# An earlier o product, wider stacked transfers and shorter layer norm sums in the first mixer of a hybrid decoder step

## The chip, the cores and the metric

The kernel runs on one core of one Trainium2 chip. The metric is the device time of one execution in microseconds (us). The time before is 1579.87 us, the median of three runs (1579.34 to 1582.29). All input weights and activations are float32.

## The reference

One inference step of a decoder trunk, for a prompt of 512 tokens and 8 samples of 8 tokens each, 576 tokens in all, d_model 1024. There are two layers, each a mixer and a convolutional FFN. The change is in the mixer of layer 0 alone:

```python
a_val, a_gate, q, k, v = split(h @ w_in)
u = a_val * sigmoid(a_gate)
c = silu(layernorm(causal_dwconv([conv_hist, u], conv_w, conv_b), ln_g, ln_b))   # 512 channels, 31 taps
q, k = partial_rope(rmsnorm(q)), partial_rope(rmsnorm(k))
o = sink_attention(q, k, v)          # window 128, 8 query heads, 2 key heads of 64
out = concatenate([c, o]) @ w_out    # 512 + 512 rows, 1024 columns
x = x + out
...
def layernorm(x, g, b):              # over the 512 channels of a token
    mu = mean(x); var = mean((x - mu)**2)
    return (x - mu) * rsqrt(var + EPS) * g + b
```

The second mixer (a Mamba-2 scan) and the two FFNs follow it and are not touched.

## The kernel before

Activations are kept with channels on the 128 partitions and tokens along the row: a tile is 128 x 576, and `HALF` names its two halves of 288 tokens. One matmul handles 128 channels of input, 128 of output, and one half.

Matmuls on weights are done with split operands. `weights()` loads 128 x 1024 weights on SP's queue (L141), ScalarE rounds them to a high part `wh` (L150), VectorE subtracts it to get the low part `wl` (L151). `split()` does the same for activations (L170 on ScalarE gives `oh`, L171 on VectorE gives `ol`). `mm3()` then issues three matmuls for each block of 128: L160 high by high, L161 high by low, L162 low by high. Results go through PSUM banks that come round in a ring, and `add_x` (L259, VectorE) adds them to the residual.

The mixer's work runs interleaved. `units()` projects the gate and value columns of the four channel blocks and q, k, v. The convolution of channel blocks 0 and 2 is done on VectorE, 31 operations of 128 x 576 for each block (`some_taps`, L436). Blocks 1 and 3 are done on TensorE by `pe_conv`: the block's `cap` (prompt) and `cas` (samples) are written to DRAM (`cad`) and read back so that four shifted copies of 32 channels stand on 128 partitions (`xp4`, `xs4`), and 64 + 64 small matmuls (L559, L566) sum the taps. `convs[1]` and `convs[3]` are these two, "conv1" and "conv3" in short. Attention goes block by block: `scores(n)` (TensorE, then the softmax on VectorE, ScalarE and GpSimd), `values(n)` (L648 transposes, L650 copies by ScalarE, L653 products, results to `of`), and `sample_scores` (L684, L688) and `sample_values` (L698 to L711) for the samples.

At the end of the mixer `of` is split into `oh` and `ol`, the layer norm of the convolution is formed from `ca[0..3]` (mean L758, variance L182, spread over the partitions L193), and the output product is done in two parts: `w_out_e[1]` times o, then `w_out_e[0]` times the normalized c, with the next norm begun in between.

A scheduler sets the order of the instructions on each engine when the program is built, from the order of the code, the dependences and its own estimates; engines then take their queues strictly in that order. All transfers stand in SP's queue, each one behind the completion of the transfer eight before it.

Of the kernel before, what the change touches and what calls it, by code (L numbers as in the profile page):

```python
# [8 lines left out]
F32 = mybir.dt.float32  # L9
# [3 lines left out]
ADD, SUB, MUL, MAX, MIN = ALU.add, ALU.subtract, ALU.mult, ALU.max, ALU.min  # L13

P = 128
NP = 512
T = 576
HB = 288
# [4 lines left out]
HALF = (slice(0, HB), slice(HB, T))  # L23
# [27 lines left out]
class Builder:  # L51
# [300 lines left out]
    def mix0(self):  # L352
        nc, d = self.nc, self.d
# [17 lines left out]
        cap, ca = {}, {}  # L371
# [3 lines left out]
        def a_gate(i):  # L375
            def go(half, p):
                if half == 0:
                    sg[i] = self.S("sg")
                    cap[i] = self.segp.tile([P, 542], F32, tag="capp", bufs=1, name="cap") if i in PC else self.S("cap", 542)
# [12 lines left out]
        cad = {i: self.dp.tile([P, 846], F32, name=f"cad{i}") for i in PC}  # L392

        def segment(i):

# [7 lines left out]
        def a_val(i):  # L403
            def go(half, p):
                s = sg[i]
                if half == 0:
                    nc.vector.tensor_tensor(cap[i][:, 30:318], p[:, :HB], s[:, :HB], op=MUL)
                else:
                    nc.vector.tensor_tensor(cap[i][:, 318:542], p[:, :224], s[:, HB:NP], op=MUL)
                    nc.vector.tensor_tensor(cas_v[i][:, :, 30:38], bt(p[:, 224:288]), bt(s[:, NP:]), op=MUL)  # L410
                    nc.sync.dma_start(d["ca_p"][i], cap[i][:, 512:542])
                    nc.sync.dma_start(d["ca_s"][i], cas_v[i][:, :, 8:38])
                    self.free(sg.pop(i))
                    if i in PC:
                        nc.sync.dma_start(cad[i][:, 0:542], cap[i])
                        nc.sync.dma_start(cad[i][:, 542:846].rearrange("p (b c) -> p b c", c=38), cas_v[i])
# [23 lines left out]
        def some_taps(n):  # L440
            for _ in range(n):
                next(taps, None)
# [94 lines left out]
        def pe_conv(i):  # L537
            w4 = [self.S("w4", NP) for _ in range(2)]
            for a in range(2):
                nc.gpsimd.tensor_tensor(w4[a].rearrange("p (k m) -> p k m", m=32),  # L540
                                        self.cv("m32", 0, 32).unsqueeze(1).broadcast_to([P, 16, 32]),
                                        self.pv("ca_wq", i * 32 + a * 16, 16).unsqueeze(2).broadcast_to([P, 16, 32]), op=MUL)
            xp4 = [self.S("xp4", 540) for _ in range(4)]
            xsp = [self.S("xs4", 608) for _ in range(2)]
            xs4 = [xsp[c // 2][:, (c % 2) * 304:(c % 2) * 304 + 304] for c in range(4)]
            src = cad[i]
            for c in range(4):
                for j in range(4):
                    n = 540 if j < 3 else 536
                    r, rc = slice(j * 32, j * 32 + 32), slice(c * 32, c * 32 + 32)  # L550
                    nc.sync.dma_start(xp4[c][r, 0:n], src[rc, j:j + n])
                    nc.sync.dma_start(xs4[c][r, 0:304 - j], src[rc, 542 + j:846])
            yield
            pp, ps = self.pm(), self.pm()
            for s in range(8):
                k = slice(0, P if s < 7 else 96)
                for c in (3, 2, 1, 0):
                    w = w4[s // 4][k, (s % 4 * 4 + c) * 32:(s % 4 * 4 + c) * 32 + 32]
                    m = nc.tensor.matmul(pp[c * 32:c * 32 + 32, :], w, xp4[c][k, 4 * s:4 * s + NP], start=s == 0, stop=s == 7)  # L559
                    if s or c < 3:  # L560
                        self.tc.keep_in_program_order(m)
            for s in range(8):
                k = slice(0, P if s < 7 else 96)
                for c in range(4):
                    w = w4[s // 4][k, (s % 4 * 4 + c) * 32:(s % 4 * 4 + c) * 32 + 32]
                    m = nc.tensor.matmul(bt(ps[c * 32:c * 32 + 32, 0:64]), w, xs4[c].rearrange("p (b t) -> p b t", t=38)[k, :, 4 * s:4 * s + 8],  # L566
                                         start=s == 0, stop=s == 7)
# [27 lines left out]
        of = []  # L595
# [81 lines left out]
        def sample_scores():  # L677
            for bh in range(2):
                p = [self.ps("sc", "sc") for _ in range(2)]
                for b4 in range(4):  # L680
                    b = bh * 4 + b4
                    for kv in range(2):
                        rows = slice(kv * 64, kv * 64 + 64)
                        nc.tensor.matmul(p[kv][b4 * 32:b4 * 32 + 32, 0:P], qs[rows, b * 32:b * 32 + 32],  # L684
                                         kct[bh][rows, b4 * P:(b4 + 1) * P], start=True, stop=True)
# [65 lines left out]
        lrs = self.S("lrs")  # L751
        csq = [self.S("csq") for _ in range(4)]
        cc = [self.pair("c") for _ in range(4)]
        for half in (0, 1):
            sl = HALF[half]
            pm = self.ps("pm")
            for i in range(4):
                nc.tensor.matmul(pm[:, :HB], self.o512, ca[i][:, sl], start=i == 0, stop=i == 3)  # L758
# [10 lines left out]
        self.free(oh, list(ca.values()), cas, lrs, csq)  # L769
# [465 lines left out]
def constants():  # L1235
# [3 lines left out]
    def put(name, a, i=0):  # L1239
        c[:a.shape[0], CV[name] + i:CV[name] + i + a.shape[1]] = a  # L1240
# [5 lines left out]
            prot[o + 8 + i, o + i] = -1.0  # L1246
            prot[o + i, o + 8 + i] = 1.0
    put("prot", prot)
    put("m32", np.tile(np.eye(32, dtype=f), (4, 1)))
# [132 lines left out]
```

## Time and profile before

| what | value |
| --- | --- |
| median of three runs | 1579.87 us |
| the profiled execution's own time | 1580.21 us |
| its span | 1578.4 us |
| TensorE's granted clock, mean | 0.997 |
| instructions | 28672 |

The profiled execution is 0.34 us above the median; 1.8 us of its time lie outside the span. Of a window's row the columns are: the window in us from the span's start, its length, then for each engine the busy time and in brackets the number of records, then the granted clock of TensorE as a share of full speed, the mean busy share of the DMA engines, and GB/s. A timeline's row has start, duration, engine, line, operation, result and operands with their shapes, the number of records, and in square brackets the idle time before the first of them and what ended it. PE is TensorE's matmul, DVE VectorE, ACT ScalarE, POOL GpSimd, SPq SP's queue of transfers.

### The profile page before, as it was taken

The page shows a single profiled execution, that of the slowest core. Times are in us where ns is not written, and L with a number is a line of the kernel's source. Part 1 is how long each engine was busy: PE and PEld are TensorE (multiplying, and loading weights), DVE is VectorE, ACT ScalarE, POOL GpSimd, SP SyncE. Part 2 cuts the span into 40 slices and gives each one's busy share as a digit, 9 for nine tenths or more (in the row PEclk, how much of TensorE's full clock was granted, in tenths as well). Part 3 has the DMA queues.
Part 4 walks back from the last instruction along what each step waited for, and adds up shares of the span by engine and source line. Part 5 has one row for each costly group of instructions (what it writes and reads, how often), then busy time and mean ns, then how long its engine had stood idle before and what let it go on. Part 6 is the DMA issues. An engine that isn't in the chain of part 4 may idle for free. (4 is left out here: it accounts for less than half of the span.)

```text
span 1578.4 us, 28672 instructions
## 1 busy us (share of the span) xinstructions
PE 1547.4 (98%) x11709; PEld 1478.0 (94%) x11709; DVE 997.7 (63%) x1750; ACT 642.0 (41%) x1197; POOL 146.9 (9%) x362
## 2 busy tenths in 40 slices
PE   8999999999999999999998999999999999999999
PEld 7966799999999999998997998998999999999998
DVE  7968586553465355677796777776975653653552
ACT  6257373221222122476765555556542321221220
POOL 0026001000000000011202002002010000000000
PEclk9999999999999999999999999999999999999999
DMA  7514223222222222225345235235322222222222
GB/s 224 127 43 111 75 69 103 87 88 81 81 80 82 93 78 76 78 83 162 122 123 163 94 106 178 94 110 171 112 81 81 81 81 81 89 77 91 81 84 76
DMA packets 69841, 157.60 MB, mean 100 GB/s; under 512 B 20158, under 2 KB 24510, under 8 KB 69710
## 3 DMA queue, kind: packets, MB, share of 16 engines
q1 hardware_dynamic: 69710, 155.77, 32.2%
q8 instruction: 92, 1.51, 0.4%
q14 instruction: 39, 0.32, 0.1%
HBM read 140.54 MB, written 15.21 MB: 99 GB/s over the span
## 5 line engine op out<-in xcount | busy, mean ns | idle before, releaser
L160 PE MATMUL mm<-hh,wh 128*128 128x288 f32 (+1 forms) x2288 | 681.6, 298 | 9.0 <-ACT wh L150 7.7
L162 PE MATMUL mm<-hh,wl 128*128 128x288 f32 x2288 | 679.9, 297 | 0.0
L161 PE MATMUL mm<-hl,wh 128*128 128x288 f32 (+1 forms) x2288 | 678.6, 297 | 0.0
L160 PEld LDWEIGHTS mm<-hh,wh 128*128 128x128 f32 (+1 forms) x2288 | 430.2, 188 | 15.1 <-ACT wh L150 8.2
L150 ACT ACTIVATE wh<-wr 128x1024 fp32r<-128x1024 f32 (+1 forms) x215 | 223.4, 1039 | 537.8 <-issue 265.4
L161 PEld LDWEIGHTS mm<-hl,wh 128*128 128x128 f32 (+1 forms) x2288 | 430.9, 188 | 2.0 <-DVE hl L360 0.3
L162 PEld LDWEIGHTS mm<-hh,wl 128*128 128x128 f32 x2288 | 429.8, 188 | 2.9 <-issue 1.5
L151 DVE TENSOR_TENSOR wl<-wr,wh 128x1024 fp32r<-128x1024 f32 (+1 forms) x215 | 259.8, 1209 | 81.5 <-ACT wh L150 81.3
L161 PE MATMUL mm<-yl,wh 128*128 128x288 f32 x960 | 287.0, 299 | 0.2 <-DVE yl L171 0.2
L160 PE MATMUL mm<-yh,wh 128*128 128x288 f32 x960 | 286.3, 299 | 0.7 <-DVE x L259 0.7
L162 PE MATMUL mm<-yh,wl 128*128 128x288 f32 x960 | 284.5, 297 | 0.4 <-DVE wl L151 0.4
L160 PEld LDWEIGHTS mm<-yh,wh 128*128 128x128 f32 x960 | 181.6, 190 | 4.3 <-DVE x L259 1.8
L161 PEld LDWEIGHTS mm<-yl,wh 128*128 128x128 f32 x960 | 182.0, 190 | 2.8 <-issue 1.4
L162 PEld LDWEIGHTS mm<-yh,wl 128*128 128x128 f32 x960 | 181.6, 189 | 1.6 <-issue 0.9
L259 DVE TENSOR_TENSOR x<-x,mm 128x288 f32<-128x288 f32 x192 | 85.3, 451 | 153.1 <-PE mm L162 152.8
L304 DVE TENSOR_TENSOR gbuf<-mm,rs 128x224 f32<-128x224 f32 x44 | 17.2, 391 | 108.9 <-PE mm L162 108.9
L315 ACT ACTIVATE gsilu<-gconv,par 128x512 f32<-128x512 f32 x44 | 31.8, 724 | 115.8 <-DVE gconv L312 115.8
L312 DVE SCALAR_TENSOR_TENSOR gconv<-gbuf,par,gconv 128x592 f32<-128x592 f32 x88 | 73.1, 831 | 1.5
L325 DVE TENSOR_TENSOR gsilu<-mm,gsilu 128x288 f32<-128x288 f32 x88 | 40.0, 455 | 50.7 <-PE mm L162 50.7
L801 DVE SCALAR_TENSOR_TENSOR cconv<-cbuf,par,cconv 128x600 f32<-128x600 f32 x72 | 60.2, 840 | 11.6 <-ACT cconv L799 10.7
L1022 ACT ACTIVATE acb<-acb,ac 128x128 f32<-128x128 f32 x128 | 41.4, 390 | 50.6 <-DMA acb<-acd 34.4
L307 POOL COPY fpo<-gbuf 128x2 f32<-128x2 f32 x44 | 12.4, 281 | 476.0 <-DVE gbuf L304 476.0
(306 smaller groups left out, 1603.1 us busy)
## 6 DMA issues: line engine op xcount, KB each, us to landing
wr<-in_w_gate SPq DMA_DIRECT2D x44, 512.0 KB, 3.3
wr<-in_w_up SPq DMA_DIRECT2D x44, 512.0 KB, 3.3
wr<-in_w_in_o SPq DMA_DIRECT2D x40, 512.0 KB, 3.4
wr<-in_w_down SPq DMA_DIRECT2D x32, 448.0 KB, 3.4
wr<-in_w_down SPq DMA_DIRECT2D x16, 512.0 KB, 3.6
acb<-acd SPq DMA_DIRECT2D x32, 256.0 KB, 4.2
h<-in_h SPq DMA_DIRECT2D x32, 256.0 KB, 3.7
out_ssm_s<-h SPq DMA_DIRECT2D x32, 256.0 KB, 2.4
```

The lines of the kernel that those rows point to most:

```text
L150: nc.scalar.activation(hi[:, :n], raw[:, :n], AF.Copy)
L151: nc.vector.tensor_tensor(lo[:, :n], raw[:, :n], hi[:, :n].bitcast(F32), op=SUB)
L160: nc.tensor.matmul(out, hi[:, ws], xh[:, sl], start=i == 0, stop=False)
L161: nc.tensor.matmul(out, hi[:, ws], xl[:, sl], start=False, stop=False)
L162: nc.tensor.matmul(out, lo[:, ws], xh[:, sl], start=False, stop=i == n - 1)
L259: nc.vector.tensor_tensor(self.x[m][:, sl], self.x[m][:, sl], p[:, :HB], op=ADD)
L304: nc.vector.tensor_tensor(g[:, 290:514], p[:, 0:224], rs[:, HB:NP], op=MUL)
L312: nc.vector.scalar_tensor_tensor(cv[:, :592], g[:, k:592 + k], w(k), cv[:, :592], op0=MUL, op1=ADD)
L315: nc.scalar.activation(sl[:, :NP], cv[:, :NP], AF.Silu, bias=b)
L325: nc.vector.tensor_tensor(sl[:, HALF[half]], p[:, :HB], sl[:, HALF[half]], op=MUL)
L801: nc.vector.scalar_tensor_tensor(cv[:, :600], g[:, k:600 + k], w(k), cv[:, :600], op0=MUL, op1=ADD)
L1022: nc.scalar.activation(acb[:, cs], acb[:, cs], AF.Relu, bias=ac[:, o:o + 1], scale=-1.0)
```

## The change

There are three parts, all in `mix0`.

First, the o product is broken up. `o_split(0)` splits the first 288 tokens of `of` ahead of the sample scores, `o_tile(m, 0)` forms output tile m for these tokens (m = 0, 1 after the sample scores, 2 to 5 after the last block's values), and the remaining tiles (m = 0 to 5 of the second half, 6 and 7 of both) come behind the layer norm's code, where all of it stood. Half 0 of `of` needs blocks 0 to 2 of the attention only.

Second, `pe_conv` reads the stacked input with 8 transfers of 128 partitions, where it had 32 of 32 partitions. Partition p now holds channel p // 4, shift p % 4; the tables `m32` and `taps4` are laid out to match, the last tap group runs over 128 rows instead of 96, and the tails of `cap` and `cad` are zeroed with two small transfers and memsets at the start.

Third, the layer norm's channel sums are made on VectorE first: `lsum` is the sum of the four `ca` tiles, and one matmul per half by `o512` gives the mean, where there were four; the squares are summed into `csq[0]`, and three variance matmuls per half replace twelve.

```diff
@@ segment tails
-                    cap[i] = self.segp.tile([P, 542], F32, ...)
+                    cap[i] = self.segp.tile([P, 543], F32, ...)
+                        nc.gpsimd.memset(cap[i][:, 542:543], 0.0)
...
+        zeros = self.Z("zeros", 3, bufs=1)
+        nc.gpsimd.memset(zeros, 0.0)
+        for i in PC:
+            nc.sync.dma_start(cad[i][:, 847:850], zeros)
@@ pe_conv
             for c in range(4):
-                for j in range(4):
-                    n = 540 if j < 3 else 536
-                    r, rc = slice(j * 32, j * 32 + 32), slice(c * 32, c * 32 + 32)
-                    nc.sync.dma_start(xp4[c][r, 0:n], src[rc, j:j + n])
-                    nc.sync.dma_start(xs4[c][r, 0:304 - j], src[rc, 542 + j:846])
+                for t, o, n in ((xp4[c], 0, 540), (xs4[c], 543, 304)):
+                    rows = cad[i][c * 32:c * 32 + 32, o:o + n]
+                    nc.sync.dma_start(t[:, 0:n], bass.AP(tensor=rows.tensor, offset=rows.offset,
+                                                         ap=[list(rows.ap[0]), [1, 4], [1, n]]))
@@ attention's end
+        oh = [self.pair("o") for _ in range(4)]
+        wo = {}
+        def o_tile(m, half):
+            if m // 2 not in wo:
+                wo[m // 2] = self.weights(d["w_out_e"][1, m // 2], 1024)
+            p = self.pm()
+            self.mm3(p[:, :HB], wo[m // 2], [(m % 2) * 4 + k for k in range(4)], oh, HALF[half])
+            self.add_x(m, half, p)
+        def o_split(half):
+            for j in range(4):
+                self.split(of[j][:, HALF[half]], oh[j], HALF[half])
+        o_split(0)
         sample_scores()
         next(convs[3])
         some_taps(5)
+        o_tile(0, 0)
+        o_tile(1, 0)
         values(3, p3)
         some_taps(5)
+        for m in range(2, 6):
+            o_tile(m, 0)
         sample_values()
         for _ in convs[3]:
             pass
         self.rings = {"mm": [2, 3, 0, 1], "aux": [4, 5, 6, 7]}
-        oh = [self.pair("o") for _ in range(4)]
-        for j in range(4):
-            self.split(of[j], oh[j])
+        o_split(1)
@@ layer norm, each half
-            for i in range(4):
-                nc.tensor.matmul(pm[:, :HB], self.o512, ca[i][:, sl], start=i == 0, stop=i == 3)
+            nc.vector.tensor_tensor(lsum[:, sl], ca[1][:, sl], ca[0][:, sl], op=ADD)
+            for i in (2, 3):
+                nc.vector.tensor_tensor(lsum[:, sl], lsum[:, sl], ca[i][:, sl], op=ADD)
+            nc.tensor.matmul(pm[:, :HB], self.o512, lsum[:, sl], start=True, stop=True)
...
                 nc.scalar.activation(csq[i][:, sl], ca[i][:, sl], AF.Square)
-            self.rstd(lrs, csq, self.o512[:, 0:1], sl)
+                if i:
+                    nc.vector.tensor_tensor(csq[0][:, sl], csq[0][:, sl], csq[i][:, sl], op=ADD)
+            self.rstd(lrs, csq[:1], self.o512[:, 0:1], sl)
...
-        self.out_proj([d["w_out_e"][1, c] for c in range(4)], oh, 4)
+        for m in range(6):
+            o_tile(m, 1)
+        for m in (6, 7):
+            for half in (0, 1):
+                o_tile(m, half)
```

The change also reorders the engines' queues. On TensorE, at the second group of sample scores (`kct` holds the samples' cached keys, `qss` their queries, `pt` transposed probabilities, `pm` the layer norm's mean, `o_101` the tile `o512`), the rows before are:

```order
L684 MATMUL sc<-kct,qss 32x128 [waits DVE_49]
L684 MATMUL sc<-kct,qss 32x128 x3
L688 MATMUL sc<-kf,qss 128x64
L648 MATMUL pt<-ident,sm 128x128 [waits Pool_49] x7
L758 MATMUL pm<-ca,o_101 128x288 [waits DVE_49]
L648 MATMUL pt<-ident,sm 128x128 [waits Activation_49]
L648 MATMUL pt<-ident,sm 128x128 x3
L758 MATMUL pm<-ca,o_101 128x288
L653 MATMUL po<-ptb,vt 64x512 [waits Activation_49]
```

After, at the same place on TensorE:

```order
L160 MATMUL mm<-oh,wh 128x288 [waits Activation_49]
L161 MATMUL mm<-ol,wh 128x288 [waits DVE_49]
L687 MATMUL sc<-kct,qss 32x128 [waits DVE_49]
L687 MATMUL sc<-kct,qss 32x128 x3
L691 MATMUL sc<-kf,qss 128x64
L162 MATMUL mm<-oh,wl 128x288
L160 MATMUL mm<-oh,wh 128x288 [waits Activation_49]
```

Eight o matmuls now stand ahead of these scores and sixteen more between them and the transposes of the last block's values (L651 after); the mean's matmuls are gone from here.

On VectorE, ahead of the sample softmax's first maximum (L605 before, L608 after; `cap` and `cas` are the gated values of channel block 3), the rows before are:

```order
L407 TENSOR_TENSOR cap<-mm,sg 128x288 [waits PE_49]
L436 SCALAR_TENSOR_TENSOR ca<-seg,par,ca 128x576 [waits DVE_49] x3
L409 TENSOR_TENSOR cap<-mm,sg 128x224 [waits PE_49]
L410 TENSOR_TENSOR cas<-mm,sg 128x8x8
L605 ISA sm,mx<-sc,cst 128x192 [waits PE_49,Pool_49]
L605 ISA mx 128x1
```

After, on VectorE:

```order
L171 TENSOR_TENSOR ol<-of,oh 128x288 [waits Activation_49,Pool_49]
L414 TENSOR_TENSOR cap<-mm,sg 128x288 [waits PE_49]
L171 TENSOR_TENSOR ol<-of,oh 128x288 [waits Activation_49,Pool_49] x2
L443 SCALAR_TENSOR_TENSOR ca<-seg,par,ca 128x576 [waits DVE_49] x2
L778 TENSOR_TENSOR lsum<-ca 128x288 [waits PE_49]
L416 TENSOR_TENSOR cap<-mm,sg 128x224 [waits PE_49]
L417 TENSOR_TENSOR cas<-mm,sg 128x8x8
L443 SCALAR_TENSOR_TENSOR ca<-seg,par,ca 128x576 [waits DVE_49]
L171 TENSOR_TENSOR ol<-of,oh 128x288 [waits Activation_49]
L608 ISA sm,mx<-sc,cst 128x192 [waits PE_49]
```

Four subtractions of the o split and the first add of `lsum` have come in ahead of the maximum; one tap (of the three that stood ahead of L407 before, by the counts from the preceding L151 on) has gone behind it.

On ScalarE, at the first projection of the mixer (`rs` is the reciprocal root of the first norm, `wh` the weights' high part), the rows before are:

```order
L184 ACTIVATE rs_r<-pt,eps 96x3 [waits PE_49] x2
L150 ACTIVATE wh<-wr 128x1024 [waits DMAHW1_49]
L197 ACTIVATE rs<-pr 128x288 [waits PE_49] x2
L150 ACTIVATE wh<-wr 128x1024 [waits DMAHW3_49,DVE_49]
L385 ACT_TABLE_LOAD
```

After, on ScalarE:

```order
L184 ACTIVATE rs_r<-pt,eps 96x3 [waits PE_49] x2
L197 ACTIVATE rs<-pr 128x288 [waits PE_49] x2
L150 ACTIVATE wh<-wr 128x1024 [waits DMAHW3_49]
L387 ACT_TABLE_LOAD
L387 ACTIVATE sg<-sg 128x288 [waits DVE_49] x2
```

The conversion that stood between L184 and L197 now follows the two copies of `rs`.

More of the change, by code (lines that the diff above doesn't have):

```diff
@@ L378, in go @@
                     sg[i] = self.S("sg")
-                    cap[i] = self.segp.tile([P, 542], F32, tag="capp", bufs=1, name="cap") if i in PC else self.S("cap", 542)
+                    cap[i] = self.segp.tile([P, 543], F32, tag="capp", bufs=1, name="cap") if i in PC else self.S("cap", 543)
+                    if i in PC:
+                        nc.gpsimd.memset(cap[i][:, 542:543], 0.0)
                     nc.gpsimd.memset(cap[i][:, 0:30], 0.0)
@@ L389, in mix0 @@
         segs = {}
+        zeros = self.Z("zeros", 3, bufs=1)
+        nc.gpsimd.memset(zeros, 0.0)
         PC, NPTB = (1, 3), 3
-        cad = {i: self.dp.tile([P, 846], F32, name=f"cad{i}") for i in PC}
+        cad = {i: self.dp.tile([P, 850], F32, name=f"cad{i}") for i in PC}
+        for i in PC:
+            nc.sync.dma_start(cad[i][:, 847:850], zeros)
         def segment(i):
@@ L414, in go @@
                     if i in PC:
-                        nc.sync.dma_start(cad[i][:, 0:542], cap[i])
-                        nc.sync.dma_start(cad[i][:, 542:846].rearrange("p (b c) -> p b c", c=38), cas_v[i])
+                        nc.sync.dma_start(cad[i][:, 0:543], cap[i])
+                        nc.sync.dma_start(cad[i][:, 543:847].rearrange("p (b c) -> p b c", c=38), cas_v[i])
                     else:
@@ L555, in pe_conv @@
             for s in range(8):
-                k = slice(0, P if s < 7 else 96)
                 for c in (3, 2, 1, 0):
-                    w = w4[s // 4][k, (s % 4 * 4 + c) * 32:(s % 4 * 4 + c) * 32 + 32]
-                    m = nc.tensor.matmul(pp[c * 32:c * 32 + 32, :], w, xp4[c][k, 4 * s:4 * s + NP], start=s == 0, stop=s == 7)
+                    w = w4[s // 4][:, (s % 4 * 4 + c) * 32:(s % 4 * 4 + c) * 32 + 32]
+                    m = nc.tensor.matmul(pp[c * 32:c * 32 + 32, :], w, xp4[c][:, 4 * s:4 * s + NP], start=s == 0, stop=s == 7)
                     if s or c < 3:
@@ L562, in pe_conv @@
             for s in range(8):
-                k = slice(0, P if s < 7 else 96)
                 for c in range(4):
-                    w = w4[s // 4][k, (s % 4 * 4 + c) * 32:(s % 4 * 4 + c) * 32 + 32]
-                    m = nc.tensor.matmul(bt(ps[c * 32:c * 32 + 32, 0:64]), w, xs4[c].rearrange("p (b t) -> p b t", t=38)[k, :, 4 * s:4 * s + 8],
+                    w = w4[s // 4][:, (s % 4 * 4 + c) * 32:(s % 4 * 4 + c) * 32 + 32]
+                    m = nc.tensor.matmul(bt(ps[c * 32:c * 32 + 32, 0:64]), w, xs4[c].rearrange("p (b t) -> p b t", t=38)[:, :, 4 * s:4 * s + 8],
                                          start=s == 0, stop=s == 7)
@@ L750, in mix0 @@
         some_taps(99)
-        lrs = self.S("lrs")
+        lrs, lsum = self.S("lrs"), self.S("lsum")
         csq = [self.S("csq") for _ in range(4)]
@@ L767, in mix0 @@
                 self.split(ca[i][:, sl], cc[i], sl)
-        self.out_proj([d["w_out_e"][1, c] for c in range(4)], oh, 4)
-        self.free(oh, list(ca.values()), cas, lrs, csq)
+        for m in range(6):
[3 more added lines that the diff above has]
+                o_tile(m, half)
+        self.free(oh, list(ca.values()), cas, lrs, lsum, csq)
         self.norm_begin("norm_f0", True)
@@ L1248, in constants @@
     put("prot", prot)
-    put("m32", np.tile(np.eye(32, dtype=f), (4, 1)))
+    put("m32", np.repeat(np.eye(32, dtype=f), 4, axis=0))
     half = np.arange(P) // 64
```

3 lines of the change are left out of this document (1 added, 2 removed).

## The prediction

> **What bounds the kernel now.** I read the engines' busy times first, then the chain that ended last, then the windows around the change, and only then single rows. The first two lines say that TensorE is busy for 98% of the span and that the chain's steps on an engine are nearly all its own.
>
> ```profile
> PE 1547.4 (98%) x11709; PEld 1478.0 (94%) x11709; DVE 997.7 (63%) x1750; ACT 642.0 (41%) x1197; POOL 146.9 (9%) x362
> PE 38%; DVE 2%; DMA 0%; ACT 0%; issue 0%; DVEq 0%; ACTq 0%
> ```
>
> So only two things can move the end: work taken from TensorE, and idle time of TensorE filled with work that it must do anyway. The windows show where the changed part has either. Their columns are sum, PE, PEld, DVE, ACT, POOL (busy us and records), granted clock, DMA share, GB/s.
>
> ```profile
> 147.96:184.57 36.61, 32.29 (x326) 21.02 (x325) 21.50 (x46) 11.71 (x32) 6.33 (x6) 0.95 0.38 83
> 184.57:206.94 22.37, 22.37 (x176) 21.75 (x177) 16.34 (x40) 15.96 (x33) 1.28 (x6) 1.00 0.14 48
> 150.00:160.00 10.00, 6.74 (x37) 3.86 (x37) 9.65 (x28) 5.86 (x15) 4.18 (x5) 0.83 0.56 90
> 300.00:320.00 20.00, 20.00 (x153) 20.00 (x152) 11.83 (x19) 5.16 (x7) 0.90 (x6) 1.00 0.24 81
> ```
>
> The first stretch (A) runs from the sample scores to the end of the last TensorE convolution ("conv3"), the second (B) on to the first matmul of c. A has the hole, at 150 to 160 with the clock down to 0.83; B is full, so there only removed work counts. The last row gives the yardstick: dense matmuls of 128x288 start every 20/153 = 0.131 us; I use 0.133.
>
> ```profile
> 149.43 0.33 PE L648 MATMUL pt<-ident,sm 128*128 128x128 f32 x1
> 150.21 0.42 PE L684 MATMUL sc<-kct,qss 64*32 64x128 f32 x8 [0.45 <-DVE mx L605]
> 150.92 0.98 PE L648 MATMUL pt<-ident,sm 128*128 128x128 f32 x7
> 156.37 1.88 PE L653 MATMUL po<-ptb,vt 128*64 128x512 f32 x4 [3.06 <-ACT ptb L650]
> 160.05 1.08 PE L653 MATMUL po<-ptb,vt 128*64 128x512 f32 x4
> 161.06 0.44 PE L698 MATMUL pt<-ident,sm 128*128 128x128 f32 x2
> 161.55 0.65 PE L758 MATMUL pm<-ca,o 128*128 128x288 f32 x2
> 162.13 0.44 PE L705 MATMUL po<-ptb,vts 64*64 64x128 f32 x4
> 163.08 0.44 PE L705 MATMUL po<-ptb,vts 64*64 64x128 f32 x4
> 165.34 0.53 PE L160 MATMUL mm<-oh,wh 128*128 128x288 f32 x2 [0.55 <-ACT oh L170]
> 176.59 7.08 PE L559 MATMUL mm<-xp,w 128*32 128x512 f32 x64
> 183.49 1.08 PE L566 MATMUL mm<-xs,w 128*32 128x64 f32 x64
> 206.94 0.29 PE L160 MATMUL mm<-ch,wh 128*128 128x288 f32 x1
> ```
>
> Before, TensorE has nothing to do while ScalarE copies the transposed probabilities (3.06 us), and the o product starts only at 165.34.
>
> **A, the o product in the hole.** Both kernels do 72 of the 192 o matmuls ahead of conv3 and 120 behind it, counted in the order of instructions, so the amount of this work is equal; its place moves by 16 us. What TensorE must do in A when nothing waits: sample scores from A's start to 149.43 and from 150.21 to 150.92, 1.46 + 0.71 = 2.17; 16 transposes by 0.107 (the third row's 0.98 less a fill, over 8) = 1.71; two value products at the rate of 160.05 to 161.06, 2.02; sample transposes 2 x 0.49 (161.06 to 161.55) and sample values 2 x 0.95 (162.13 to 163.08) = 2.88; 72 o matmuls by 0.133 = 9.58; conv3 from 176.59 to 184.57 = 7.98. Sum 26.34. The twelve mean records that before has here go (part B).
>
> To that come waits. The new one is at the second sample scores, queued on TensorE behind eight o matmuls, for a bank that VectorE's first maximum releases. Ahead of that maximum VectorE now does four o subtractions and one sum, and one tap fewer:
>
> ```profile
> 149.80 0.34 DVE L605 CUSTOM_DVE_ANT_0 sm<-sc,cst 128x192 f32<-128x192 f32 x1
> 206.54 0.82 DVE L171 TENSOR_TENSOR cl<-ca,ch 128x288 fp32r<-128x288 f32 x2
> 188.26 0.45 DVE L259 TENSOR_TENSOR x<-x,mm 128x288 f32<-128x288 f32 x1
> 146.17 3.28 DVE L436 SCALAR_TENSOR_TENSOR ca<-seg,par,ca 128x576 f32<-128x576 f32 x3
> 154.26 0.81 DVE L436 SCALAR_TENSOR_TENSOR ca<-seg,par,ca 128x576 f32<-128x576 f32 x1
> 138.42 9.34 POOL L616 TENSOR_SCALAR sm<-sm,den 128x256 f32<-128x256 f32 x8 [5.32 <-DVE den L614]
> ```
>
> 4 x 0.41 + 0.45 - 1.0 = 1.1 later, so the maximum ends near 151.2 to 151.7 and not at 150.14. TensorE is there at 149.43 + 8 x 0.133 = 150.5: a wait of 0.7 to 1.2, taken 1.1. What stands behind it (the second scores, then 16 o matmuls, then the transposes) moves along; nothing on ScalarE needs it sooner. The remaining waits (the sample probabilities' copies, the second value product) I set at 0.9, between nothing and what is left of before's: 36.61 less 26.34, less twelve mean records by 0.65/2, less the waits shown (3.06 + 0.45 + 0.55) and the 0.8 that the slow value product lost, 1.5. A then takes 26.34 + 2.0 = 28.4 in place of 36.61: **-8.2**.
>
> The rows of taps carry a choice. A tap takes 0.81 alone, and 3.28/3 = 1.09 while GpSimd's multiplications run, each 9.34/8 = 1.17. The five new two-input operations stand in that stretch too, so they cost up to 0.28 more each, 1.4 in all; that is the upper end of 1.1 to 1.6 in the step above. [...]
>
> **B, the layer norm's sums.** Removed from TensorE:
>
> ```profile
> L182 PE MATMUL pt<-o,csq x48: 164/223/244, 186.3 to 194.6; 128*96 128x1 f32 x48
> 188.17 1.61 PE L182 MATMUL pt<-o,csq 128*96 128x1 f32 x18
> 189.64 0.38 PE L162 MATMUL mm<-oh,wl 128*128 128x288 f32 x1
> L758 PE MATMUL pm<-ca,o x16: 405/406/510, 151.7 to 185.4; 128*128 128x288 f32 x16
> 184.54 1.24 PE L758 MATMUL pm<-ca,o 128*128 128x288 f32 x4
> 192.71 0.65 PE L193 MATMUL pr<-dg,ones 96*128 96x288 f32 x2
> ```
>
> A full-precision matmul stands as two records. The 48 variance records become 12; one takes (189.64 - 188.17)/18 = 0.082. The last four mean records stay as two halves of two, 1.1 together. B dense: 120 x 0.133 = 15.96, means 1.1, variances 12 x 0.082 = 1.0, the two spreads of rstd 2 x 0.5 (0.65 less a fill) = 1.0, sum 19.0; the same sum with 48 records gives 22.0 for a measured 22.37, so I add 0.4: 19.4, **-2.95**. VectorE gains five or six adds by 0.45 per half, of which one per half runs already in A. They lengthen the norm's chain, which TensorE covers with the 120 o matmuls. Before, the last c piece was ready at 206.54 + 0.82 = 207.36, that is 22.8 behind the end of conv3; after, the first tile of half 1 wants that piece 19.4 + 21 x 0.133 = 22.2 behind it. The chain loses 36 records and part of its waits behind TensorE, and gains up to 5 us of adds if none lies beside ScalarE's squares. Walking it with before's durations I get 22.0; the cost is 0 to 5.6, taken 0 since nearly every add stands beside a square.
>
> **The stacked taps.** 24 DMA issues go from SP's queue for each of the two convolutions.
>
> ```profile
> 156.52 0.32 SPq L551 DMA_DIRECT2D xp<-cad  x1
> 171.73 0.42 SPq L552 DMA_DIRECT2D xs<-cad  x1
> xp<-cad SPq DMA_DIRECT2D x12, 67.5 KB, 1.9
> cad<-cap SPq DMA_DIRECT2D x1, 271.0 KB, 5.6
> ```
>
> Before, 32 issues took 15.6 us and the last landed near 174, which conv3 at 176.59 did not feel. After, TensorE reaches conv3 near 169.0, so with the old transfers it would have had to wait 5 us: the wider ones pay here. They move 1.73 MB; the window of 150 to 160 shows 90 GB/s with the DMA engines 0.56 busy, 160 GB/s if full, so 11 us when nothing else runs and they land near 167.5. Cost 0, with some 1.5 us to spare.
>
> **The beginning.** The two small zero transfers stand early on SP's queue, ahead of the second pair of weight loads, and the scheduler moves one ScalarE conversion of gate weights behind two copies (L197).
>
> ```profile
> 15.01 1.85 SPq L141 DMA_DIRECT2D wr<-in_w_in_e  x2
> wr<-in_w_in_e SPq DMA_DIRECT2D x4, 512.0 KB, 6.7
> 23.98 1.05 ACT L150 ACTIVATE wh<-wr 128x1024 fp32r<-128x1024 f32 x1
> 25.06 1.23 DVE L151 TENSOR_TENSOR wl<-wr,wh 128x1024 fp32r<-128x1024 f32 x1 [0.41 <-ACT wh L150]
> 25.73 0.29 PE L162 MATMUL mm<-hh,wl 128*128 128x288 f32 x1
> ```
>
> Two issues of 0.9 move these loads to 16.86, and they land near 23.5 by the second row (which is of 10 to 24 us), just ahead of 23.98: 0, at most 1. The conversion now takes the slot of 23.98; its low part is done on VectorE at 25.06 + 1.23 = 26.29, and TensorE wants it at 25.73: **+0.65** (0 if ScalarE finds an earlier slot, 1.2 if the loads or the copies come later). Changes between kinds of matmul cost about 0.1 each in the rows of B (0.38 where 0.29 is normal); the new order has some eight more: **+0.8**.
>
> **Sum.** -8.2 - 2.95 + 0.65 + 0.8 = -9.7. The profiled execution took 1580.21, 0.34 above the median of the runs shown; 1580.21 - 9.7 = 1570.5. Bounds: waits in A from nothing to 3.5, hand-overs 0 to 1.5, beginning 0 to 1.2, which is a gain of 7 to 12.5 for this case, 1567.7 to 1573.2.
>
> **Rivals.** (1) Half the gain is lost on VectorE. Either each of the five new operations waits for a whole GpSimd instruction, 5 x 1.17 = 5.9 (1576.4), or the norm's adds all lie on its chain, 5.6 (1576.1). For it: VectorE is 9.65 of 10 busy at 150 to 160. Against it: taps lost 0.28 each, and 16 us of matmuls lie over the norm. 12%. (2) No change: both of these together, 11.5 against 9.7, so 1582. The step then only shifts its waits. 5%. (3) Slower: the wide transfers land late, and conv3, which stands in TensorE's queue ahead of the 120 remaining o matmuls, waits with nothing to cover it. It decides from a landing at 169.0 + 9.7 = 178.7, 22 us for eight transfers. If they went one by one at the pace of the last row above (5.6 for 271 KB), 1.73 MB would take 36 us, land at 192 and give 1594. Against it: 12 transfers of 67.5 KB landed in 1.9 each while issued 0.46 apart, so they overlap. 4%.
>
> **How the numbers follow.** The first case has 79%, and its middle is the prediction. The range 1566.5 to 1576.5 adds the upper rival's two prices and one us below for waits that the sum overstates; it leaves out (2), (3) and some of the tails, near 15%. A gain below 0.2%, 3.2 us, can't be told from no change here. Faster gets 0.90, from the first case and nearly all of (1), same 0.05, slower 0.05.
>
> **What the changed profile would show.** Right: the 3.06 wait at the value product gone; the first o matmul near 149.5; the granted clock of 150 to 160 near 1.0; a wait near 1 us on TensorE at the second sample scores; conv3 starting near 169 and the first c matmul near 197; 12 variance records; the eight wide transfers issued within 4 us and landed before 168. Wrong: a wait of TensorE ahead of conv3 for a DMA (3), waits at o matmuls for the subtraction or above 2 us at the scores (1), or idle time at the first c tiles for VectorE (1 and 2).

## The result, and the profile after

The changed kernel takes 1568.26 us (median of four runs, 1567.04 to 1569.66) against 1579.77 for the kernel before on the same chip; the ratio is 0.9928 with a 95% interval of 0.9914 to 0.9942, so 11.5 us faster where 9.4 were forecast (1570.5, range 1566.5 to 1576.5). The profiled execution took 1567.04 us with a span of 1565.3, 13.1 less than the profiled one of before.

The first fence has windows of the changed kernel: the prediction's stretches A (sample scores to the end of conv3) and B (to the first c matmul), then C (to the last c matmul), the ten microseconds that held the hole, and 340 us of dense work in the last FFN. The second fence has C and the dense work of the kernel before.

```profile
148.98:177.47 28.49, 28.13 (x313) 18.66 (x312) 22.82 (x54) 11.32 (x33) 7.90 (x7) 1.00 0.41 101
177.47:196.96 19.49, 19.03 (x140) 18.60 (x141) 18.11 (x45) 15.04 (x31) 0.30 (x3) 1.00 0.17 55
196.96:223.95 26.99, 26.94 (x204) 26.60 (x203) 23.30 (x52) 18.13 (x38) 1.72 (x11) 1.00 0.28 86
150.00:160.00 10.00, 9.68 (x80) 8.05 (x73) 9.55 (x30) 5.84 (x16) 5.52 (x6) 1.00 0.59 100
1205.00:1545.00 340.00, 340.00 (x2564) 339.80 (x2564) 172.26 (x265) 83.14 (x107) 8.78 (x52) 1.00 0.27 84
```

```profile
206.94:233.91 26.97, 26.86 (x204) 26.51 (x203) 22.58 (x50) 17.57 (x36) 0.88 (x8) 1.00 0.24 80
1218.00:1558.00 340.00, 340.00 (x2558) 339.79 (x2557) 171.79 (x263) 82.14 (x107) 8.76 (x52) 1.00 0.27 84
```

A fell from 36.61 to 28.49 (-8.1), B from 22.37 to 19.49 (-2.9), C is unchanged. A begins 1.0 later (148.98 against 147.96). That is 10.0 up to the last c matmul. The other 3.0 lie behind it, in layers that the change does not touch: six more matmuls fit into 340 us. The hole is gone and the clock there is 1.00, not 0.83.

TensorE's rows of the changed kernel: the wait at the beginning, what is left of waiting in the mixer, and the variance's records.

```profile
25.29 0.40 PE L162 MATMUL mm<-hh,wl 128*128 128x288 f32 x1 [0.46 <-DVE wl L151]
150.44 0.40 PE L160 MATMUL mm<-oh,wh 128*128 128x288 f32 x1
151.48 0.29 PE L161 MATMUL mm<-ol,wh 128*128 128x288 f32 x1
152.10 0.42 PE L687 MATMUL sc<-kct,qss 64*32 64x128 f32 x8 [0.33 <-DVE mx L608]
166.99 1.04 PE L563 MATMUL mm<-xp,w 128*32 128x512 f32 x2
177.93 0.75 PE L781 MATMUL pm<-lsum,o 128*128 128x288 f32 x2 [0.46 <-DVE lsum L780]
196.96 0.30 PE L160 MATMUL mm<-ch,wh 128*128 128x288 f32 x1
L182 PE MATMUL pt<-o,csq x12: 164/223/223, 182.6 to 188.7; 128*96 128x1 f32 x12
```

The o product starts at 150.44, 15 us sooner. The wide transfers, as the DMA view of 150 to 178, the view of their line (both convolutions) and SP's queue have them:

```profile
xp<-cad SPq DMA_DIRECT2D x4, 270.0 KB, 3.5
DMA to landing us min/median/max: 2.9/3.5/4.4
156.68 0.56 SPq L556 DMA_DIRECT2D xp<-cad  x1
161.50 0.60 SPq L556 DMA_DIRECT2D xs<-cad  x1
```

The last of the eight is issued at 161.50 and has the longest way, 4.4, so it lands at 165.9. Conv3 begins at 166.99 with two matmuls; the rest of it starts at 169.51, behind the sample values.

### The profile page after: what moved, and what is told of

It is laid out like the page before. It is cut to its first block, busy times and chain, and to the rows that moved or that the text cites. A ratio compares the mean times of both kernels' runs of the same rounds, so it can differ in the third digit from the quotient of the medians.

```text
span 1565.3 us, 28515 instructions
## 1 busy us (share of the span) xinstructions
PE 1538.9 (98%) x11661; PEld 1471.1 (94%) x11661; DVE 1002.2 (64%) x1766; ACT 642.3 (41%) x1201; POOL 148.5 (9%) x365
## 5 line engine op out<-in xcount | busy, mean ns | idle before, releaser
L162 PE MATMUL mm<-hh,wl 128*128 128x288 f32 x2288 | 681.5, 298 | 1.0 <-DVE wl L151 1.0
L161 PE MATMUL mm<-hl,wh 128*128 128x288 f32 x2288 | 678.2, 297 | 0.0
L162 PEld LDWEIGHTS mm<-hh,wl 128*128 128x128 f32 x2288 | 430.6, 188 | 4.8 <-issue 2.0
L161 PEld LDWEIGHTS mm<-hl,wh 128*128 128x128 f32 x2288 | 432.0, 189 | 2.6 <-DVE hl L171 0.6
L151 DVE TENSOR_TENSOR wl<-wr,wh 128x1024 fp32r<-128x1024 f32 (+1 forms) x215 | 260.1, 1210 | 82.0 <-ACT wh L150 81.9
L162 PE MATMUL mm<-yh,wl 128*128 128x288 f32 x960 | 283.3, 296 | 0.3 <-DVE wl L151 0.3
L162 PEld LDWEIGHTS mm<-yh,wl 128*128 128x128 f32 x960 | 180.4, 188 | 1.5 <-issue 0.9
```

The costliest lines, as they stand in the source:

```text
L151: nc.vector.tensor_tensor(lo[:, :n], raw[:, :n], hi[:, :n].bitcast(F32), op=SUB)
L161: nc.tensor.matmul(out, hi[:, ws], xl[:, sl], start=False, stop=False)
L162: nc.tensor.matmul(out, lo[:, ws], xh[:, sl], start=False, stop=i == n - 1)
```

## The experiments

The kernels of this section are given by their A, B and C windows. Between the first 15 us and the last matmul, a drop of the granted clock to one half lasts 3.41 us or a multiple of it in these traces (at 156.51, 842.59 and 1091.76 in the kernel before, at 738.04 and 847.27 in the changed one, each 3.41 at a clock of 0.50), and 3.41 cost up to 1.7. A window's loss by it is at most its length times what its clock lacks of 1.

**Each part taken out of the changed kernel, and each part put alone into the kernel before.**

```diff
@@ no_o, against after
-        o_split(0)
-        o_tile(0, 0)
...
+        for j in range(4):
+            self.split(of[j], oh[j])
...
+        self.out_proj([d["w_out_e"][1, c] for c in range(4)], oh, 4)
@@ no_transfers, against after
-                for t, o, n in ((xp4[c], 0, 540), (xs4[c], 543, 304)):
+                for j in range(4):
+                    nc.sync.dma_start(xp4[c][r, 0:n], src[rc, j:j + n])
+                    nc.sync.dma_start(xs4[c][r, 0:304 - j], src[rc, 542 + j:846])
@@ no_sums, against after
-            nc.tensor.matmul(pm[:, :HB], self.o512, lsum[:, sl], start=True, stop=True)
+            for i in range(4):
+                nc.tensor.matmul(pm[:, :HB], self.o512, ca[i][:, sl], start=i == 0, stop=i == 3)
-            self.rstd(lrs, csq[:1], self.o512[:, 0:1], sl)
+            self.rstd(lrs, csq, self.o512[:, 0:1], sl)
```

`transfers_alone`, `sums_alone` and `o_alone` are the kernel before with the second, the third and the first part of the change.

> The o product back behind the layer norm's code; the wide transfers and the summed layer norm stay. In this kernel's order the last convolution stands ahead of all 192 o matmuls, so nothing fills the hole ahead of the value product (3 us) but the convolution comes sooner. Theory: dense work up to the convolution's end is 26.3 - 9.6 = 16.8, plus some 7 us of waits, so it ends near 173 and the first c matmul follows 192 x 0.133 + 3.5 = 29 us later, near 202, against 196.96 in the changed kernel: some 5 us slower than it, near 1573.5. Rival: the early o product carries the whole 8.1 us of stretch A, then near 1576.5.

Measured: 1575.42 us (ratio to before 0.9963, 0.9948 to 0.9979).

```profile
150.07:176.45 26.38, 21.09 (x241) 9.95 (x240) 20.52 (x45) 11.77 (x32) 6.65 (x6) 0.81 0.42 108
176.45:205.51 29.06, 28.59 (x213) 28.16 (x213) 23.29 (x55) 16.20 (x33) 2.25 (x6) 1.00 0.19 61
158.46 1.98 PE L656 MATMUL po<-ptb,vt 128*64 128x512 f32 x4 [3.09 <-ACT ptb L653]
166.43 1.07 PE L563 MATMUL mm<-xp,w 128*32 128x512 f32 x8 [1.50 <-DMA xp<-cad]
```

The hole is back (3.09, TensorE busy for 21 of 26 us) with three drops of the clock in a row (0.81), and here the wide transfers are waited for, 1.50. A + B is 55.4, 7.5 more than after. The theory holds for B, 29.06 where 29 were expected. A took 26.4, not 16.8 + 7: the wait for the transfers was not expected, and the drops (26.38 x 0.19 = 5.0, part of it in idle time) are large enough for the rest. In sum the loss lies nearer the rival's 8.1 than the theory's 5, and the time (1573.5 or 1576.5) does not tell them apart.

> The 32 narrow transfers back; the early o product and the summed layer norm stay. In this kernel's order 139 o matmuls stand ahead of the last convolution and 53 behind it. Theory: the transfers are not waited for, but the norm's chain (22 us behind the convolution) has only 53 x 0.133 + 3 = 10 us of work over it, so TensorE waits 4 to 9 us at the first c tiles: 1572 to 1577. Rival 1: the narrow transfers are hidden, as in the kernel before, and cost nothing: 1568.3. Rival 2: the convolution waits 5 us or more for a DMA.

Measured: 1572.87 us (0.9951, 0.9936 to 0.9967).

```profile
147.43:186.58 39.15, 37.82 (x380) 28.93 (x379) 27.25 (x61) 13.43 (x35) 7.87 (x7) 0.96 0.41 100
186.58:200.28 13.70, 9.97 (x72) 9.33 (x72) 13.22 (x32) 9.79 (x19) 0.30 (x3) 0.94 0.11 38
200.28:230.22 29.94, 29.89 (x204) 29.26 (x205) 24.68 (x57) 21.13 (x48) 1.95 (x11) 0.91 0.18 60
PE mm L160 <- ACT ch L170: 3.3, 1, 3.3
```

No transfer is waited for. TensorE waits for the layer norm, 3.3 us, as 139 of the o matmuls have gone ahead of conv3 and do not cover it any more; a drop begins in this wait, and C, at a clock of 0.91, is 3.0 us longer. The theory holds in kind, with a wait under the 4 to 9 that it gave. By the windows both rivals fall (A + B + C is 7.8 longer than after); the time's interval overlaps that of the changed kernel at its edge (0.9936 to 0.9942).

> Mean by four matmuls and variance by twelve per half again; the early o product and the wide transfers stay. Theory: with the hole filled by o, the means no longer lie in it; all 16 mean records stand behind the convolution, so 12 x 0.27 to 0.32 = 3.2 to 3.9 for the means and 36 x 0.082 = 2.95 for the variances come back: +6 to +7 on the changed kernel, near 1574.7. Rival: only the 2.95 that the prediction's part B counted, near 1571.2.

Measured: 1575.63 us (0.9970, 0.9959 to 0.9981).

```profile
149.00:177.08 28.08, 28.05 (x314) 18.70 (x313) 21.25 (x49) 11.42 (x33) 6.79 (x7) 1.00 0.43 109
177.08:205.20 28.12, 28.12 (x188) 26.98 (x189) 17.23 (x41) 16.03 (x33) 1.41 (x6) 0.88 0.06 20
```

B is 8.6 longer than after, A 0.4 shorter. TensorE is busy throughout, but the clock is 0.88: 28.12 x 0.12 = 3.4 is lost to two drops, and the 5.2 left are the twelve mean and 36 variance records (6 to 7 expected). So the rival falls. The prediction's 2.95 is only the variance's share; it had booked the twelve mean records in A, at 12 x 0.65/2 = 3.9. With no hole for them to lie in, they cost nearly their full time.

> The kernel before with the 8 wide transfers and nothing else. In its order the last convolution moves ahead of all o matmuls. Theory: it starts near 165 where the o product started before; TensorE's idle time ahead of it stays, only the short waits for the o split (0.55 + 0.3) go, so 0.5 to 2 us faster than before, 1578 to 1579.3. Rival: the transfers carry a large part of the gain by themselves, 1575 or less.

Measured: 1580.58 us (0.9998, 0.9989 to 1.0008).

```profile
148.55:172.52 23.97, 20.47 (x248) 10.47 (x247) 18.75 (x40) 11.68 (x32) 6.32 (x6) 0.93 0.49 126
172.52:207.19 34.67, 34.67 (x256) 33.87 (x255) 20.78 (x47) 15.95 (x33) 1.11 (x6) 0.95 0.15 47
```

Conv3 ends 12 us sooner and the o product follows it; A + B stays 58.6 (before 59.0). By the interval at most 0.1% is gained alone, the low end of what was expected or less.

> The kernel before with the layer norm's sums on VectorE and nothing else; 72 o matmuls stand ahead of the last convolution as before. Theory: B loses 2.95 us of variance records; of A's twelve mean records four lay in the hole and eight in dense work, 8 x 0.3 = 2.4, if the convolution's transfers (landed near 174) allow it: 1575 to 1577. Rival: the transfers of the stacked taps become the bound and only B's 2.95 is gained, or the norm's chain does and nothing is.

Measured: 1573.28 us (0.9957, 0.9939 to 0.9974).

```profile
147.81:184.77 36.96, 30.94 (x313) 20.71 (x312) 23.22 (x51) 11.68 (x32) 6.63 (x6) 0.91 0.34 77
184.77:205.03 20.26, 19.25 (x141) 18.69 (x141) 18.17 (x42) 14.46 (x26) 0.30 (x3) 1.00 0.17 53
1210.00:1550.00 340.00, 340.00 (x2572) 339.78 (x2571) 172.52 (x266) 83.32 (x107) 8.72 (x52) 1.00 0.26 84
```

B loses 2.1 and A nothing: with the mean's records gone, TensorE just stands idle longer (30.94 busy of 36.96, before 32.29 of 36.61) and the clock drops twice. The longest wait in A is again that for ScalarE's copies (3.6 us, 3.06 before); none is for a transfer. So neither the 2.4 that the theory put in A nor the rivals' reasons are there. The time is lower than 1575 to 1577 all the same, and the third row says where: 2572 matmuls in 340 us against 2558.

> The kernel before with the early o product and nothing else. In its order 136 o matmuls stand ahead of the last convolution and 56 behind it. Theory, after the run without the wide transfers: the hole is filled, but the norm's chain has only 56 x 0.133 + 7 = 14.5 us of work over it and TensorE waits for it; 1577 to 1581, no gain that can be measured. Rival: the early o product alone gives the 3 us of the hole or more, 1576 or less.

Measured: 1571.23 us (0.9940, 0.9919 to 0.9961).

```profile
146.52:185.42 38.90, 38.87 (x390) 29.22 (x389) 25.80 (x56) 13.55 (x35) 6.79 (x7) 1.00 0.43 106
185.42:199.03 13.61, 13.61 (x114) 13.05 (x113) 9.05 (x23) 9.11 (x19) 1.11 (x6) 1.00 0.13 40
199.03:226.67 27.64, 27.48 (x204) 26.79 (x203) 25.45 (x59) 21.33 (x48) 1.27 (x8) 1.00 0.18 59
```

The theory fell and the rival holds: TensorE is full nearly throughout, with no drop in these windows. The layer norm up to the first c matmul fits under 13.6 us of matmuls here; in no_transfers it takes 13.7 as well, but TensorE has only 10.0 of work beside it. So the chain that I had put at 22 us behind conv3 was in good part waiting for its turn behind o matmuls, not work.

Put together, A + B + C and what the clock lacked in them:

| kernel | A + B + C | lost to the clock, at most | left |
| --- | --- | --- | --- |
| before | 85.95 | 1.7 | 84.2 |
| transfers_alone | 85.7 | 3.4 | 82.3 |
| sums_alone | 83.7 | 3.4 | 80.3 |
| o_alone | 80.15 | 0 | 80.15 |
| no_sums (o, transfers) | 83.2 | 3.4 | 79.8 |
| no_transfers (o, sums) | 82.8 | 5.1 | 77.7 |
| no_o (transfers, sums) | 82.5 | 5.1 | 77.4 |
| after | 75.0 | 0 | 75.0 |

In the raw column the parts do not add: the transfers gain 0.3, the sums 2.2 and o 5.8 alone, each pair 2.8 to 3.5, all three 11.0. With the drops taken out the three nearly do: 1.9 + 3.9 + 4.1 = 9.9 alone, 9.2 together, though the pairs still miss the sums of their parts by 1.0 to 1.6, one above and two below. So much of the difference may be the clock's. How much is not shown: each row is one profile, and the third column is an upper bound, since a drop may lie in TensorE's idle time. By the times alone o_alone (0.9919 to 0.9961) is not told from the changed kernel; the windows tell them apart.

**The same kernel again, and two places where time was left.**

> The changed kernel once more, without an edit: what another profiled execution of it shows. Theory: the stretches of the mixer come back within 0.2 us (A 28.5, B 19.5), and the stretch behind the mixer, which was 3.0 us shorter than in the kernel before though the change does not touch it, differs by one or two us from the 1337.45 of the first profile, by as many drops of the granted clock (1.7 us each) as it happens to have. Rival: that stretch comes back at 1337 to 1338, so its gain belongs to the new order of the instructions.

Measured: 1565.77 us (0.9916, 0.9899 to 0.9933); A 28.48, B 19.50.

```profile
149.01:177.49 28.48, 28.15 (x313) 18.68 (x312) 22.80 (x54) 11.31 (x33) 7.88 (x7) 1.00 0.40 101
177.49:196.99 19.50, 19.04 (x142) 18.60 (x141) 18.12 (x45) 15.04 (x31) 0.30 (x3) 1.00 0.16 55
```

The mixer repeats within 0.02 us. The stretch behind it is 1336.11 (last c matmul to the last matmul of the output), 1.3 shorter than in the first profile and one drop of the clock fewer (the one at 847.3). Without drops both have 1334.0 to 1334.4, the kernel before 1337.1 with as many drops as the first. Four more profiles with both the early o product and the sums give 1333.6 to 1335.3. So the theory holds: the drops move the time from run to run, and the 3 us belong to the kernel.

> The last attention block's probabilities are multiplied by 1/sum on ScalarE, not on GpSimd, so GpSimd no longer runs beside VectorE's taps, o subtractions and sums. Theory from the rows (1.09 us beside GpSimd, 0.81 alone): the taps between 140 and 149 fall to 0.81, the first maximum of the sample scores comes 1 to 2 us earlier, the 0.49 wait of TensorE at the second sample scores goes; 0.3 to 0.6 us faster than the changed kernel. Rival (each operation stops for a whole GpSimd instruction): the o subtractions were 1 us longer each and the gain is 2 us or more. Third: ScalarE's eight copies delay the o split and it is slower.

```diff
-                nc.gpsimd.tensor_scalar(t, t, den[:, i:i + 1], None, op0=MUL)
+                nc.scalar.activation(t, t, AF.Copy, scale=den[:, i:i + 1])     # last block only
```

Measured: 1568.06 us (0.9925, 0.9912 to 0.9937); A 28.15, that is 0.34 less, B the same. The wait at the second scores is gone, as expected. The time does not show the gain (1565.77 for the kernel without the edit in the same set of runs). Why the wait was there is in VectorE's and GpSimd's rows of the changed kernel (first fence) and of this one:

```profile
150.46 1.30 DVE L171 TENSOR_TENSOR ol<-of,oh 128x288 fp32r<-128x288 f32 x1
146.60 0.81 DVE L171 TENSOR_TENSOR ol<-of,oh 128x288 fp32r<-128x288 f32 x2
150.06 2.61 POOL L547 TENSOR_TENSOR w<-cst,par 128x512 f32<-128x512 f32 x2
```

```profile
143.35 2.77 DVE L443 SCALAR_TENSOR_TENSOR ca<-seg,par,ca 128x576 f32<-128x576 f32 x2
142.75 2.75 POOL L547 TENSOR_TENSOR w<-cst,par 128x512 f32<-128x512 f32 x2 [9.22 <-PE mm L161]
```

Beside GpSimd's multiplications (one tensor input) a subtraction took 0.41 as always. The last one, beside the making of conv3's weights (two tensor inputs, 1.3 each), took 1.30: it ended 0.3 after the first of these. With the multiplications gone, the weights were made at 142.75 and slowed two taps there (1.38 each, 0.82 alone). So the edit moved this cost to a place where TensorE does not wait; it did not remove it.

> The two zero transfers stand beside the write of the gated values, not at the start. ScalarE's order at the first projection is then that of the kernel before (conversion, two copies, conversion). Theory: the wait of TensorE for the low part of the weights at 25.3 (0.46 us and a hand-over) goes, and the sample scores start 0.6 us sooner; 1567.6. Rival: the wait was covered by the later waits for the loads, and nothing changes.

```diff
+                        nc.sync.dma_start(cad[i][:, 847:850], zeros)   # beside the write of cap and cas
-            nc.sync.dma_start(cad[i][:, 847:850], zeros)               # at the start
```

Measured: 1567.13 us (0.9917, 0.9904 to 0.9930); the wait at 25.3 is gone, and A begins at 147.11, not at 148.98 and 149.01: 1.9 sooner where 0.6 was expected. Four more profiles with the early zero transfers have A's start at 148.55 to 150.07, the seven without at 146.52 to 148.02. The time itself does not tell this kernel from the changed one (1565.77 in the same set of runs).

> Both edits on the changed kernel. Theory: they add, 0.9 to 1.2 us faster than it, near 1567.2. Rival: the noise of the clock drops hides it, or only one of them counts.

Measured: 1564.85 us (0.9909, 0.9894 to 0.9923), the lowest median of all: A begins at 147.41 and takes 28.15, and the last c matmul is done at 222.04, 1.9 before the changed kernel's. Its intervals overlap with after_again's; that it beats the changed kernel is read from the profiles, not from the times.

**The layers behind the mixer.**

```diff
-        self.free(cc)
+        self.free(cc); self.idle = self.idle[20:] + self.idle[:20]
```

> The kernel before; only the list of idle buffers is turned by 20 places at the end of the first mixer, so that the layers behind it get other buffers. Every instruction of TensorE, VectorE and ScalarE stands in the same place. In the traces so far dense matmuls of the last 360 us start every 132.95 ns in the two kernels with the old o product and the old sums, 132.68 with the early o product alone, 132.22 with the new sums alone, 132.61 with both, the same in every profile of one kernel. Theory: which buffers the later layers get sets this rate, so it moves by 0.1 ns or more here too, and the stretch behind the mixer by 1 us or more, either way. Rival: the buffers don't matter (the rate comes from the order of instructions or the size of the program), and it stays at 132.9 to 133.0.

Measured: 1579.33 us (1.0001, 0.9990 to 1.0012).

```profile
1217.00:1557.00 340.00, 340.00 (x2563) 339.81 (x2563) 172.21 (x264) 83.05 (x106) 8.75 (x52) 1.00 0.27 84
147.06:182.78 35.72, 32.72 (x326) 21.75 (x325) 21.58 (x46) 11.83 (x32) 6.46 (x6) 0.95 0.36 80
182.78:208.20 25.42, 25.42 (x177) 24.80 (x178) 16.40 (x40) 15.95 (x33) 0.10 (x1) 0.87 0.13 43
```

> The same turn by 20 places on the kernel with both edits (late zero transfers, probabilities on ScalarE). Theory: its dense rate, 132.61 before, moves by 0.1 ns or more as well, either way, with the mixer's stretches as they were (28.15, 19.50). Rival: it stays within 0.05 ns.

Measured: 1566.90 us (0.9917, 0.9902 to 0.9931).

```profile
1208.00:1548.00 340.00, 340.00 (x2559) 339.80 (x2559) 171.40 (x263) 82.36 (x105) 8.76 (x52) 1.00 0.26 84
```

The edit changes nothing but the buffers of the later layers, and the dense rate moved both times: 2563 matmuls in 340 us where the kernel before has 2558 (132.70 ns between starts, 132.95 before), and 2559 on the other kernel (132.87, 132.61 before). TensorE, VectorE and ScalarE run the same instructions in the same order. On SP's queue a few loads and on GpSimd a few copies and fills of the first FFN changed places, all before 243 us; the rate is measured behind 1200 us, where all orders are equal. The theory holds for the rate. The stretch behind the mixer, drops taken out, is 1.6 shorter in slots_before; in slots_both the dense layers lost 1.5 and the second mixer gained as much. What about the place of a buffer sets the rate was not tried.

## Why the prediction was right

**A.** -8.2 forecast, -8.1 measured, and after_again repeats it. The total holds, but its term of 2.0 for waits was made of something else. TensorE is busy for 28.13 of the 28.49. The wait at the second sample scores was 0.5 (151.48 + 0.13 to 152.10) and not 1.1: the first maximum ended 3.1 behind A's start where 3.2 to 3.7 was worked out. The 72 o matmuls took 0.6 more than 9.58, at the changes between kinds of matmul. The last 1.0 lies between the sample transposes and the end of conv3 (11.9 for 2.88 + 7.98), where two conv3 matmuls now stand among the sample values. That these come to about 2.0 as well is in part luck.

**VectorE beside GpSimd.** The step averaged three taps beside GpSimd to 1.09 and concluded that each operation loses 0.28. The row held two taps of 0.80 and 0.92 beside multiplications and one of 1.49 beside the two-input operation. Of the five new operations four lost nothing (0.41 to 0.45 each) and one lost 0.9: the last subtraction, 1.30 for 0.41, beside the two-input operation of 150.06 to 151.45. Beside the one-input multiplications VectorE lost next to nothing. GpSimd did lose there: in the kernel before, a multiplication that took 0.92 with VectorE idle (at 124.70) took 2.02 beside the weights' subtraction (L151, 1.21, at 141.90). No run shows the 5 x 1.17 = 5.9 us of the upper rival, a whole GpSimd instruction for each of the five: it was wrong by its count.

**B.** -2.95 forecast, -2.88 measured; the first c matmul at 197 forecast, 196.96 measured. At the c tiles the norm's chain cost nothing, as taken; at its start TensorE waits 0.46 for the first `lsum` (the row at 177.93), which no step had. The whole of this part was booked as 2.95 here and 3.9 for the mean in A, 6.9. Taking the sums out of the finished kernel costs 5.2 on TensorE and up to 3.4 more by the clock (no_sums), while alone, beside the hole, they gained nothing in A (sums_alone).

**The stacked taps.** Forecast as issued within 4 us and landed near 167.5, 1.5 us ahead of the need. They were issued in 4.8 and landed by 165.9, 1.1 ahead of conv3's first matmul, which came 2 us sooner than forecast. The 1.73 MB took 9.2 us where the row of before gave 11. The forecast that the old transfers would cost 5 us beside the early o product, by a wait of conv3, was wrong in its way: the order puts other o matmuls ahead of conv3, and the wait comes at c (no_transfers).

**The beginning.** The wait came where it was put (L162 at the sixth block, 0.46 and a hand-over), but the term was mis-sized: 0.65 forecast, and 1.9 given back when the zero transfers move. The 1.0 between the two profiles understates it, because in the one of before TensorE came late to its full rate (starts 0.24 apart up to 12.99, 0.13 from 13.21 on): from 10 to 14 us it holds 19 matmuls, where `after` and `late_zeros` hold 26. `slots_before`, the same instructions as before up to there, holds 27 and begins A 0.9 sooner (147.06). Over all profiles A begins at 149.07 in the mean with the early zero transfers and at 147.42 without. The wait explains 0.6; where the rest arises, between 26 and 79 us, is open.

**The hand-overs.** The +0.8 for changes between kinds of matmul is not there on top of the others: A and B come out at 28.5 and 19.5, with 28.4 and 19.4 worked out without it. The changes do cost time (0.6 at A's o matmuls), but A's 2.0 and the 0.4 added in B already held it.

**What no step had.** The sum was -9.7, and up to the last c matmul the profiles give -10.0. This nearness is in part luck: the hand-overs were counted twice, and the dearer beginning is hidden by the late full rate in the profile of before. The last 3 us of the profile come from dense matmuls behind the mixer, 0.34 ns each: the change shifts the rotation of the buffers (one buffer more for `lsum`, other places for the o tiles). That buffers move the rate by as much is shown by the two turned kernels; that they make up all of the 0.34 is inferred. With them the two profiled times differ by 13.2, beyond the 12.5 of the prediction's first case, whose bounds add up to 13.1 when redone; the medians differ by 11.5. Kernels fall into groups by these two parts alone: 132.95 with neither, 132.68 with the early o, 132.22 with the sums, 132.61 with both, whatever the transfers.

## What to carry to other kernels

When the bound engine has holes, look at what lies in them before pricing what is taken out: the mean's matmuls were partly free in the hole and cost nearly their full time once it was filled, so one part's price depends on the others. Judge a change of one per cent by stretches of the trace and not by the total alone: the mixer repeated within 0.02 us while totals of the same kernel ran from 1563.0 to 1571.6. And before explaining a gain in untouched layers, turn the buffers' rotation and see if it comes and goes.

## What the runs showed of the hardware

In these runs a drop of the clock needed no idle engine. The kernel before and slots_before have the same instructions in B, yet B took 22.37 in the one and 25.42 in the other, both with TensorE busy throughout, at clocks of 1.00 and 0.87. In slots_before the first drop (187.81 to 191.22) follows right behind 18 variance records of one column each:

```profile
186.39 1.66 PE L182 MATMUL pt<-o,csq 128*96 128x1 f32 x18
188.30 0.44 PE L160 MATMUL mm<-oh,wh 128*128 128x288 f32 x1
188.00:192.00 4.00, 4.00 (x21) 4.00 (x21) 0.89 (x3) 2.31 (x5) 0.00 (x0) 0.60 0.00 0
```

Matmuls stand 0.24 apart there instead of 0.13. Of the five kernels with 48 such records three had drops in B in the profiled execution, five drops in all, and each of the five begins within 0.3 us of the end of a run of 18 or 20 of these records. Five more such runs had no drop behind them. With 12 records B has a clock of 1.00 in five profiles (after, after_again, no_o, sums_alone, act_probs) and of 0.94 in no_transfers, where the drops began in a 3.3 us wait. So the short matmuls are the likely cause; no run varies their number alone. Why a drop lasts 3.41 us, and why one execution has it where another with the same instructions has none, is not shown.

The other is the dense rate. The same matmuls in the same order started 132.95 or 132.70 ns apart, and 132.61 or 132.87, depending on which buffers their operands lie in. Over all kernels the rate runs from 132.2 to 133.0, and profiles of the same group agree to 0.01 ns.
